# Products and running sums of the later modulation: from VectorE to ScalarE and GpSimd

## The chip, the cores and the metric

The kernel runs on one core of one Trainium2 chip. A core has five engines with a queue each: TensorE (PE, matrix products; its weight loads are shown apart as PEld), VectorE (DVE), ScalarE (ACT), GpSimd (POOL) and SyncE (SP), which here issues nearly all DMA transfers. Every engine executes its queue in order. Matrix products are written to PSUM; the other data lie in SBUF.

The metric is the time of one execution on the device, in microseconds (us); lower is better.

## What is computed

Two decoder layers over 512 tokens of width 2048, in float32. Both take shift, scale and gate from a conditioning vector `c`; the matrices for this are the *modulation* matrices. Cut to what matters:

```python
def reference(x, c, w_mod, b_mod, ...):
    c_act = jax.nn.silu(c)
    for l in range(DEPTH):                                  # 2 layers
        mod = c_act @ w_mod[l] + b_mod[l]                   # (1, 2048) @ (2048, 6144)
        shift, scale, gate = jnp.split(mod, 3, axis=-1)
        h = x * (1.0 + scale[:, None]) + shift[:, None]
        if l < N_A:                                         # layer 0
            y = diff_attention(h, a_w_in[l], a_w_out[l], ...)
        else:                                               # layer 1
            if kv is None:
                kv = shared_kv(x, c_act, kv_w_mod, kv_b_mod, kv_w, kv_b_f)
            k_sh, v_sh, F_sh = kv
            y = forgetting_attention(h, b_w_in[l - N_A], b_w_out[l - N_A], k_sh, v_sh, F_sh)
        x = layer_norm(DN_ALPHA * x + gate[:, None] * y, ln_g[l], ln_b[l])
    return x
```

`shared_kv` has a modulation of its own (`c_act @ kv_w_mod`, 2048 x 4096). A modulation is a vector times a matrix: each of the 2048 rows of the matrix is scaled by one number and the rows are added up.

## The kernel before

**Projections.** Nearly all of the time is matrix products of 512 tokens with weight matrices, done by `group`. The weights of a projection of 512 columns come in eight pairs of k-tiles (a k-tile is 128 of the 2048 rows). `WeightStream` loads a pair into `wst` (four buffers, L46, issued on SP), ScalarE rounds it to a shorter float `whi` (L93), and VectorE forms the rest `wlo = wst - whi` (L94); each of the two has three buffers. A product is then three matmuls (L173, L174, L175): upper by upper, upper by lower, lower by upper. For every pair, `group` goes over four blocks of tokens or features (`burst`: six matmuls); so a projection has 32 bursts. After a burst, `tick` takes one step of waiting work out of the list `pieces` (the attention of the head before) and, where `bg` says so, one step of `background`.

**The modulation.** The shift and scale of layer 0 are needed first and are found in the start stage (L476 and around it, up to about 165 us); that part is not edited. All later modulation goes through `mod_stream`, twice:

- the first stream, in layer 0: its gate, the shift and scale of `shared_kv` and the shift of layer 1, 16 segments of 512 columns. Tiles `ms` of two k-tiles (512 KB), two buffers, one loaded ahead;
- the second stream, during the shared values and keys (`vj[1]` to `vj[3]`, then `kj[0]` to `kj[3]`): the scale and gate of layer 1, 8 segments. Tiles `ms` of one k-tile (256 KB), three buffers, two loaded ahead.

A segment has 16 steps, one for each k-tile: VectorE multiplies a 128x512 tile with a column of silu(c) (`cact`, one number a partition) and adds it to `macc` in one instruction (L386); the first step of a segment only multiplies (L384). `macc` has two buffers. When a segment is summed, `mod_row` rounds it into `mhi` (ScalarE, L168) and `mlo` (VectorE, L169), two matmuls with ones add up its 128 partitions (L406, L407), VectorE adds the bias (L408), and the row goes to DRAM (L409).

`bg` takes a step after every second burst in the `vg` projections, after two of three in `qk`, `vj[2]`, `vj[3]` and `kj`, and after every burst in the last 17 of `vj[1]`. So the first stream has 24 - 8 = 16 segments, 256 steps, and the second 8 segments, 128 steps.

**Order.** SP takes the loads of `ms` (L369), of the weights (L46) and the stores of values (L978) in one queue. A load into a buffer that is still in use holds up those behind it. Each step of `mod_stream` first issues the load for a later step and then computes its own. The text gives priorities; the order on each engine is set when the program is compiled, by a planner that goes by estimated times and free buffers, except on VectorE in the start stage, where the order is as written.

**Work around the streams that the prediction speaks of.** In layer 0 the attention of a head runs in pieces between the bursts: scores, maximum on VectorE (L699), exponential on ScalarE (L703), transposes (L720), values, then `norm`: ScalarE copies the output (L746) and squares it (L749), VectorE takes a reciprocal root in about ten small steps (L246 to L255) and scales `og` (L753), and TensorE transposes `og` (L767). In the values' projections ScalarE copies each result into `vt` (two buffers, L977), which SP stores to DRAM (L978); there are four such copies at the end of each projection. The keys' projections copy into tiles of their own (L971) and store nothing.

Of the kernel before, what the change touches and what calls it, by code (L numbers as in the profile page):

```python
# [12 lines left out]
AF = mybir.ActivationFunctionType  # L13
ALU = mybir.AluOpType
# [4 lines left out]
T = 512  # L19
# [8 lines left out]
# Order of the start, see there: c sums of modulation, m their columns, t a k-tile of h, l its lower part,  # L28
# s a split of weights, g products of a k-tile, digits so many steps of the modulation's sums.
# [4 lines left out]
class Job:  # L34
    """A projection: runs of columns of a 2048-row weight matrix."""
# [14 lines left out]
class WeightStream:  # L50
    """Loads weights two k-tiles at a time and splits them into two float32r parts, ahead of their
    products."""
# [26 lines left out]
    def step(self, extra=None):  # L79
        """Splits the next two k-tiles; extra gives tiles for them outside the stream's own."""  # L80
        job, s = self.order[self.done]
        self.load(self.done + 1)
        st = self.stage[self.done]
        w = job.width
        if extra:
            hi, lo = ([extra() for _ in range(2)] for _ in range(2))
            for k in range(2):
                self.nc.scalar.copy(hi[k][:, :w], st[:, k, :w])
                self.nc.vector.tensor_tensor(lo[k][:, :w], st[:, k, :w], hi[k][:, :w].bitcast(F32), op=ALU.subtract)
        else:  # L90
            hi = self.pool.tile([P, 2, 512], F32R, name="whi", tag="whi", bufs=3)
            lo = self.pool.tile([P, 2, 512], F32R, name="wlo", tag="wlo", bufs=3)
            self.nc.scalar.copy(hi[:, :, :w], st[:, :, :w])  # L93
            self.nc.vector.tensor_tensor(lo[:, :, :w], st[:, :, :w], hi[:, :, :w].bitcast(F32), op=ALU.subtract)  # L94
            hi, lo = ([t[:, k, :] for k in range(2)] for t in (hi, lo))
        self.subs[(id(job), s)] = (hi, lo)
        self.done += 1
# [12 lines left out]
def tile_yoco(  # L110
# [24 lines left out]
    V, S, PE, G = nc.vector, nc.scalar, nc.tensor, nc.gpsimd  # L135
# [35 lines left out]
    def products(dst, lhs, rhs, start, stop):  # L171
        """dst += lhs^T rhs with lhs and rhs as (hi, lo) parts."""
        PE.matmul(dst, lhs[0], rhs[0], start=start, stop=False)  # L173
        PE.matmul(dst, lhs[0], rhs[1], start=False, stop=False)  # L174
        PE.matmul(dst, lhs[1], rhs[0], start=False, stop=stop)  # L175

    # ---------------------------------------------------------------- constants
# [11 lines left out]
    # rows of parameters, turned into columns by the tensor engine  # L189
# [51 lines left out]
    def rsqrt(y, v, n, pool):  # L241
        """y = v ** -0.5 by Newton steps from an estimate on the exponent."""
# [14 lines left out]
    # ---------------------------------------------------------------- weight order  # L257
# [3 lines left out]
    # the first two heads: all but the keys of the second component, which follow for both at once  # L261
    first = {h: (Job(a_w_in, [(256 * h, 256), (2048 + 256 * h, 128)]), vg[h]) for h in range(2)}
    kk = Job(a_w_in, [(2048 + 128, 128), (2048 + 384, 128)])
    # k-tiles whose modulation is found together, and the order in which the two heads take k-tiles
# [6 lines left out]
    # the last columns for half of the tokens first, whose LayerNorm is then done ahead of the end  # L271
# [34 lines left out]
    def group(job, natural, evac, banks=range(4), bg=0, before_sub=None, after_sub=None, hold=0, after_held=None):  # L306
        """One projection; natural: tokens on the partitions, else features. The last hold weights
        stay until each bank has had them, one bank after the other."""
# [41 lines left out]
    # modulation vectors as columns [feature, k-tile]  # L350
# [4 lines left out]
    def mod_stream(segs, new_stage, new_acc, nk):  # L355
        """Vector-engine products of silu(c) with columns of a modulation matrix, 512 columns a
        segment; yields after each k-tile."""
# [17 lines left out]
        for k, (i, r) in enumerate(todo):  # L375
# [4 lines left out]
            for kk in range(nk):  # L380
                kt = nk * r + kk
                w = t[:, kk, :] if nk > 1 else t
                if kt == 0:
                    V.tensor_scalar(acc, w, cact[:, 0:1], None, op0=ALU.mult)  # L384
                else:
                    V.scalar_tensor_tensor(acc, w, cact[:, kt : kt + 1], acc, op0=ALU.mult, op1=ALU.add)  # L386
                if kt == KT - 1:
                    summed.append(segs[i][2](acc))
                if kt in (1, 5) and summed:
                    if next(summed[0], None) is None:  # L390
                        summed.pop()
                yield
# [3 lines left out]
    def mod_row(pool, ones_r, dst, bias, one):  # L396
        """Sums over the partitions, as ones^T acc with acc in two parts; in two steps."""
# [14 lines left out]
    # ---------------------------------------------------------------- start: modulation and first projections  # L412
    # Shift and scale of sets of k-tiles: sums over silu(c) on the vector engine, for the first sets
    # half of them on the tensor engine. Each k-tile is multiplied for both heads; a head's partial
    # sums wait in SBUF while the other one's are in PSUM.
    part = {}
    with tc.tile_pool(name="start", bufs=2, reuse_waits="tile") as sp, tc.manual_schedule(engines={ET.DVE}):
# [12 lines left out]
        # one entry a tile: set, first k, number of k  # L430
# [53 lines left out]
        def dv(n):  # L484
            """n more products of modulation, none of them past the set after those summed."""
# [138 lines left out]
    # ---------------------------------------------------------------- layer 0: differential attention  # L624
# [182 lines left out]
    # head 1 waits until head 0 is done, and with it the values and gates of head 2  # L807
# [29 lines left out]
    # ---------------------------------------------------------------- output projections and LayerNorm  # L837
# [12 lines left out]
    def out_projection(jobs, layer, zp, opened, residual, norm, after_held=None):  # L850
        """z = residual + gate * y with the statistics of its rows; norm(b) follows a block's last
        columns. zp is filled by opened() once the pieces of the last head have been traced."""
# [43 lines left out]
    # h = x1 * scale + shift on n^T: x1 = n * g + b  # L896
# [19 lines left out]
    def build_half(s, half):  # L916
        """k-tiles 2s and 2s+1 of h for the keys and values, tokens of one half."""
# [17 lines left out]
        # the transposed tokens take the place of the others  # L935
# [3 lines left out]
    # the first values: the tokens of the second half are behind those of the first, which are ready earlier  # L939
# [25 lines left out]
    # ---------------------------------------------------------------- shared keys, values and forget gates  # L965
# [18 lines left out]
    # for each k-tile 64 columns: the two parts of the weights in columns 0-15 and 32-47. The products  # L984
    # take 128 columns, of which those 64 count.
# [26 lines left out]
    def forget_sums():  # L1012
        """-cumsum(min(z, 0) - log1p(exp(-|z|)))"""
# [6 lines left out]
        # log1p(e) = log(w) + (e - (w - 1)) / w  # L1020
# [63 lines left out]
    # ---------------------------------------------------------------- layer 1: forgetting attention  # L1084
# [4 lines left out]
    # the last block of keys is multiplied from query 256 on, so that its rows have 256 columns  # L1089
# [127 lines left out]
    # ---------------------------------------------------------------- layer 1: output projection and LayerNorm  # L1217
# [81 lines left out]
```

## Time and profile before

| | |
|---|---|
| time, median of 3 runs | 2016.39 us (2015.3 to 2018.02) |
| profiled execution, first to last instruction | 2017.1 us |
| mean granted TensorE clock | 0.994 of full speed |
| steps of `mod_stream` on VectorE | 360 of 750 ns and 24 of 485 ns |
| loads of `ms` | 128 of 512 KB (first stream), 128 of 256 KB (second) |
| first and last step, both streams | start at 176.7 and at 1320.5 us |

The page of the profile gives the busy time of each engine over the execution and, in further views, over any stretch. A row of a group reads: line, engine, operation, output<-inputs, shape, count, then busy time in all and the mean of one in ns, then how long the engine stood idle just before these instructions and what ended that. Waits are given as total us, number, longest. TensorE's busy time is modelled from its issue, so the number of matmuls in a stretch tells more than the share. The lines themselves are in the prediction.

### The profile page before, as it was taken

How to read it: one execution, taken by the hardware profiler on the slowest of the kernel's cores; microseconds unless marked ns; L12 is line 12 of the kernel's file. 1: busy time of each engine (PE TensorE's matmuls, PEld its weight loads, DVE VectorE, ACT ScalarE, POOL GpSimd, SP SyncE). 2: the span in 40 equal slices, each digit the busy share in tenths (PEclk: the TensorE clock that was granted, in tenths of full speed). 3: DMA queues.
4: the chain of work that ended last, by engine and by line, in shares of the span. 5: the costliest groups of instructions: out<-in, count | busy, mean ns of one | idle time of the engine just before them, and what ended most of it. 6: DMA issues, size and time to landing. Idle time of an engine off the chain costs nothing.

```text
span 2017.1 us, 25055 instructions
## 1 busy us (share of the span) xinstructions
PE 1967.3 (98%) x9115; PEld 1627.0 (81%) x9115; DVE 1335.3 (66%) x2435; ACT 722.2 (36%) x1230; POOL 2.2 (0%) x10
## 2 busy tenths in 40 slices
PE   5999999999999999999999999999999999999997
PEld 4888878888878888888878877888888888888885
DVE  6887878777667677853575666645455555576678
ACT  2422444423333334431263222224333333453232
POOL 0000000000000000000000000000000000000000
PEclk8999999999999999999999999999999999999999
DMA  9994755564556565452344878733233323232754
GB/s 343 343 316 143 243 172 162 163 224 156 190 167 209 166 221 184 156 165 94 115 138 141 260 255 261 261 124 127 92 102 96 103 91 103 95 118 90 259 193 175
DMA packets 263095, 353.79 MB, mean 175 GB/s; under 512 B 18022, under 2 KB 162556, under 8 KB 262204
## 3 DMA queue, kind: packets, MB, share of 16 engines
q1 hardware_dynamic: 262896, 352.18, 53.3%
q8 instruction: 71, 1.16, 0.2%
q14 instruction: 52, 0.43, 0.1%
q10 hardware_dynamic: 76, 0.02, 0.0%
HBM read 339.47 MB, written 12.66 MB: 175 GB/s over the span
## 4 chain that ended last, share of the span: by engine, by line
PE 81%; DMA 8%; DVE 8%; issue 1%; SPq 1%; ACT 1%; DVEq 0%; ACTq 0%
PE acc L173 23%; PE acc L175 23%; PE acc L174 23%; DMA ms<-in_w_mod_dram 5%; DVE macc L386 2%; DVE wlo L94 2%; PE sc L174 2%; PE sc L175 2%; PE sc L173 2%; DMA sms<-in_w_mod_dram 1%; PE o L175 1%; PE o L174 1%; PE o L173 1%; PE tr L1163 1%; DMA ms<-in_kv_w_mod_dram 1%
## 5 line engine op out<-in xcount | busy, mean ns | idle before, releaser
L93 ACT CAST whi<-wst 128x1024 fp32r<-128x1024 f32 (+2 forms) x339 | 349.6, 1032 | 685.4 <-PE acc L175 315.6
L94 DVE TENSOR_TENSOR wlo<-wst,whi 128x1024 fp32r<-128x1024 f32 (+2 forms) x339 | 404.6, 1196 | 279.9 <-ACT whi L93 265.7
L173 PE MATMUL acc<-whi,hh 128*128 128x512 f32 x1252 | 494.6, 398 | 4.4 <-ACT vt L977 2.9
L174 PE MATMUL acc<-wlo,hh 128*128 128x512 f32 x1252 | 490.6, 392 | 0.1
L175 PE MATMUL acc<-whi,hl 128*128 128x512 f32 x1252 | 489.5, 391 | 0.0
L173 PE MATMUL acc<-hh,whi 128*128 128x512 f32 x1184 | 469.0, 396 | 3.6 <-ACT vt L977 2.9
L174 PE MATMUL acc<-hl,whi 128*128 128x512 f32 x1184 | 462.3, 390 | 0.0
L175 PE MATMUL acc<-hh,wlo 128*128 128x512 f32 x1184 | 462.3, 390 | 0.0
L386 DVE SCALAR_TENSOR_TENSOR macc<-ms,cact,macc 128x512 f32<-128x512 f32 x360 | 270.0, 750 | 116.2 <-DMA ms<-in_w_mod_dram 83.7
L173 PEld LDWEIGHTS acc<-whi,hh 128*128 128x128 f32 x1252 | 236.3, 189 | 51.5 <-ACT vt L977 4.2
L175 PEld LDWEIGHTS acc<-whi,hl 128*128 128x128 f32 x1252 | 235.8, 188 | 51.1 <-DVE hl L934 0.3
L174 PEld LDWEIGHTS acc<-wlo,hh 128*128 128x128 f32 x1252 | 236.2, 189 | 44.3 <-DVE wlo L94 0.5
L173 PEld LDWEIGHTS acc<-hh,whi 128*128 128x128 f32 x1184 | 222.6, 188 | 48.4 <-ACT vt L977 4.1
L175 PEld LDWEIGHTS acc<-hh,wlo 128*128 128x128 f32 x1184 | 222.5, 188 | 48.0
L174 PEld LDWEIGHTS acc<-hl,whi 128*128 128x128 f32 x1184 | 222.8, 188 | 41.1
L476 DVE SCALAR_TENSOR_TENSOR sacc<-sms,cact,sacc 128x512 f32<-128x512 f32 (+1 forms) x127 | 89.5, 705 | 5.9 <-DMA sms<-in_w_mod_dram 2.2
L1152 ACT ACTIVATE eb<-eb,mnb 128x128 f32<-128x128 f32 (+1 forms) x64 | 36.1, 564 | 96.7 <-DVE mnb L1149 95.6
L703 ACT ACTIVATE e<-e,mn 128x128 f32<-128x128 f32 (+3 forms) x64 | 36.1, 563 | 88.7 <-DVE mn L699 88.1
L1149 DVE CUSTOM_DVE_ANT_0 eb<-sc,biasb 128x128 f32<-128x128 f32 (+1 forms) x64 | 31.4, 490 | 52.8 <-PE sc L175 52.8
L1167 DVE TENSOR_TENSOR pTl<-tr,pTh 128x128 fp32r<-128x128 f32 (+1 forms) x64 | 31.2, 487 | 26.5 <-ACT pTh L1166 26.1
L1166 ACT CAST pTh<-tr 128x128 fp32r<-128x128 f32 (+1 forms) x64 | 27.1, 424 | 43.6 <-PE tr L1163 42.9
L769 ACT ACTIVATE ogT<-tr,subg 128x128 f32<-128x128 f32 x64 | 20.0, 364 | 56.0 <-PE tr L767 56.0
(251 smaller groups left out, 1740.0 us busy)
## 6 DMA issues: line engine op xcount, KB each, us to landing
wst<-in_a_w_in_dram SPq DMA_DIRECT2D x240, 256.0 KB
ms<-in_w_mod_dram SPq DMA_DIRECT2D x64, 512.0 KB
ms<-in_kv_w_mod_dram SPq DMA_DIRECT2D x64, 512.0 KB
wst<-in_kv_w_dram SPq DMA_DIRECT2D x64, 512.0 KB
ms<-in_w_mod_dram SPq DMA_DIRECT2D x128, 256.0 KB
wst<-in_b_w_in_dram SPq DMA_DIRECT2D x128, 256.0 KB
sms<-in_w_mod_dram SPq DMA_DIRECT2D x56, 512.0 KB
wst<-in_b_w_out_dram SPq DMA_DIRECT2D x48, 512.0 KB
```

Source lines behind the costliest of these rows:

```text
L93: self.nc.scalar.copy(hi[:, :, :w], st[:, :, :w])
L94: self.nc.vector.tensor_tensor(lo[:, :, :w], st[:, :, :w], hi[:, :, :w].bitcast(F32), op=ALU.subtract)
L173: PE.matmul(dst, lhs[0], rhs[0], start=start, stop=False)
L174: PE.matmul(dst, lhs[0], rhs[1], start=False, stop=False)
L175: PE.matmul(dst, lhs[1], rhs[0], start=False, stop=stop)
L386: V.scalar_tensor_tensor(acc, w, cact[:, kt : kt + 1], acc, op0=ALU.mult, op1=ALU.add)
L476: V.scalar_tensor_tensor(acc, w, sc, acc, op0=ALU.mult, op1=ALU.add)
L703: S.activation(e[:, :w], e[:, :w], AF.Exp, bias=mn, scale=-1.0, accum_out=rs)
L1149: V.tensor_tensor_reduce(out=e[:, :w], in0=sc[:, :w], in1=bias[:, :w], scale=-1.0, scalar=3.0e38, op0=ALU.add, op1=ALU.min, accum_out=mn)
L1152: S.activation(e[:, :w], e[:, :w], AF.Exp, bias=mn, scale=-1.0, accum_out=rs)
L1166: S.copy(pTh[:, 0 : i + 1, ts], src)
L1167: V.tensor_tensor(pTl[:, 0 : i + 1, ts], src, pTh[:, 0 : i + 1, ts].bitcast(F32), op=ALU.subtract)
```

## The change

In `mod_stream`, ScalarE forms the product, in place of the loaded tile, and GpSimd adds it to `macc`. The first product of a segment is written to `macc` by ScalarE. Loads, buffers, `mod_row`, the order of the text and all else stay; the rest of the diff takes out comments.

```diff
@@ mod_stream
             for kk in range(nk):
                 kt = nk * r + kk
                 w = t[:, kk, :] if nk > 1 else t
                 if kt == 0:
-                    V.tensor_scalar(acc, w, cact[:, 0:1], None, op0=ALU.mult)
+                    S.activation(acc, w, AF.Copy, scale=cact[:, 0:1])
                 else:
-                    V.scalar_tensor_tensor(acc, w, cact[:, kt : kt + 1], acc, op0=ALU.mult, op1=ALU.add)
+                    S.activation(w, w, AF.Copy, scale=cact[:, kt : kt + 1])
+                    G.tensor_tensor(acc, acc, w, op=ALU.add)
                 if kt == KT - 1:
                     summed.append(segs[i][2](acc))
```

## The prediction

> **What bounds the kernel now.** I read the page first, then the stretches of the two streams that the change touches, then TensorE's waits in them, then who waits for the modulation's tiles, then the chain.
>
> ```profile
> span 2017.1 us, 25055 instructions
> ...
> PE 1967.3 (98%) x9115; PEld 1627.0 (81%) x9115; DVE 1335.3 (66%) x2435; ACT 722.2 (36%) x1230; POOL 2.2 (0%) x10
> ```
>
> TensorE is idle for 50 us in all, about 22 of them in the first stretch, ahead of any edited line. VectorE is off the bound on average, and so the 282 us that leave it are not a gain of that size. By stretch (span, then PE, PEld, DVE, ACT, POOL busy, clock, DMA share, GB/s):
>
> ```profile
> 0.00:50.00 50.00, 28.34 (x126) 22.91 (x127) 34.83 (x63) 11.78 (x15) 1.60 (x9) 0.90 1.02 343
> ...
> 160.00:400.00 240.00, 235.95 (x1128) 194.94 (x1127) 183.25 (x408) 100.98 (x217) 0.56 (x1) 1.00 0.56 180
> 400.00:640.00 240.00, 238.47 (x1109) 197.92 (x1109) 162.42 (x307) 82.06 (x152) 0.00 (x0) 1.00 0.59 190
> 640.00:860.00 220.00, 219.60 (x1041) 182.85 (x1040) 164.72 (x347) 88.68 (x176) 0.00 (x0) 1.00 0.56 181
> ...
> 1090.00:1180.00 90.00, 87.07 (x384) 70.94 (x383) 57.52 (x70) 21.26 (x26) 0.00 (x0) 1.00 0.75 242
> 1180.00:1250.00 70.00, 67.14 (x294) 54.55 (x293) 45.61 (x58) 16.45 (x19) 0.00 (x0) 1.00 0.80 260
> 1250.00:1330.00 80.00, 80.00 (x353) 65.94 (x352) 52.85 (x69) 21.54 (x25) 0.00 (x0) 1.00 0.72 238
> ```
>
> The first row is that start. The first stream (layer 0) runs in the next three rows, the second in the last three. TensorE's idle time is 4.05 + 1.53 + 0.40 = 6.0 us in the first and 2.93 + 2.86 + 0 = 5.8 us in the second. These 11.8 us are the most that the change can win. Three views of TensorE's waits (165 to 400, 540 to 600, 1085 to 1250 us) name them:
>
> ```profile
> PE tr L767 <- DVE og L753: 3.1, 3, 1.3
> ...
> PE tr L767 <- DVE og L753: 1.0, 1, 1.0
> ...
> PE acc L173 <- ACT vt L977: 5.8, 5, 2.7
> ```
>
> In layer 0 it is VectorE, late with the gated head `og`: 4.1 us. In the second stream it is ScalarE, late with `vt`; the views of all waits, and the same for 1060 to 1330 us, say why:
>
> ```profile
> ACT vt L977 <- DMA v_dram<-vt: 16.2, 4, 7.4
> DVE macc L386 <- DMA ms<-in_w_mod_dram: 83.7, 69, 3.4
> DVE macc L386 <- DMA ms<-in_kv_w_mod_dram: 26.3, 28, 3.2
> ...
> DVE macc L386 <- DMA ms<-in_w_mod_dram: 61.0, 45, 3.4
> ...
> SPq L369 <- DVE macc L386: 166.2, 189, 4.6
> ```
>
> `vt` has two buffers; the third copy waits for the store of the first, and that store stands on SP's queue behind loads of `ms` (L369) that wait for VectorE to free a buffer. So the second stream's TensorE time is already lost to the ring of `ms` buffers: load, use, free, load. VectorE itself stood 110.0 us waiting for `ms`, 61.0 of them in the second stream. In layer 0 the chain shows what that does (start, us, what):
>
> ```profile
> 261.29 1.22 DVE wlo L94
> ...
> 263.79 4.64 DMA ms<-in_w_mod_dram
> 268.45 0.75 DVE macc L386
> ...
> 273.41 0.50 DVE og L753
> ...
> 274.05 0.41 PE tr L767 x2
> ```
>
> The sum stands 4.64 us for its tile at VectorE's head, the small steps of `og` stand behind it, and TensorE behind them.
>
> **The change, part by part.** It removes 360 fused steps and 24 first products from VectorE:
>
> ```profile
> L386 DVE SCALAR_TENSOR_TENSOR macc<-ms,cact,macc 128x512 f32<-128x512 f32 x360 | 270.0, 750 | 116.2 <-DMA ms<-in_w_mod_dram 83.7 <-DMA ms<-in_kv_w_mod_dram 26.3 <-DVE mn L699 0.3
> L384 DVE TENSOR_SCALAR macc<-ms,cact 128x512 f32<-128x512 f32 x24 | 11.6, 485 | 6.0 <-DMA ms<-in_w_mod_dram 5.5
> L94 DVE TENSOR_TENSOR wlo<-wst,whi 128x1024 fp32r<-128x1024 f32 (+2 forms) x339 | 404.6, 1196 | 279.9 <-ACT whi L93 265.7 <-DMA vld<-v_dram 8.4 <-DMA wst<-in_kv_w_dram 2.5
> ```
>
> That is 281.6 us. It adds 384 products on ScalarE and 360 sums on GpSimd. No row has either; the nearest are these:
>
> ```profile
> L168 ACT CAST mhi<-macc 128x512 fp32r<-128x512 f32 x24 | 14.9, 620 | 40.4 <-PE tr L406 23.3 <-DVE macc L386 17.1
> L769 ACT ACTIVATE ogT<-tr,subg 128x128 f32<-128x128 f32 x64 | 20.0, 364 | 56.0 <-PE tr L767 56.0
> L1166 ACT CAST pTh<-tr 128x128 fp32r<-128x128 f32 x16 | 4.2, 264 | 7.1 <-PE tr L1163 6.9
> L522 ACT ACTIVATE htmp<-tr,mcol 128x512 f32<-128x512 f32 x16 | 12.3, 770 | 0.0
> ...
> L646 POOL IOTA dist<- 128x512 f32 x1 | 0.6, 560 | 158.7 <-DVE sacc L476 158.7
> ```
>
> *A product.* The copy of such a tile takes 620 ns; a scale taken from a column costs 364 - 264 = 100 ns more. I take 0.72 us, between 0.62 and the 0.77 of an instruction with two such columns. In all 276 us. In layer 0 ScalarE goes from 101 + 82 + 89 = 272 us of 700 to 272 + 256 x 0.72 = 456 (65%), VectorE from 510 to 510 - 256 x 0.75 = 318; in the second stream ScalarE goes from 59 of 240 to 151. Neither is full, so as sheer work the products are hidden behind TensorE; uncovered, they would cost their 276 us.
>
> *A sum.* GpSimd's only row of the size is the IOTA, one pass of writing: 0.56 us. An add reads two operands and writes one. Below I put one pass (0.56, all overlapped), above three (1.68), and take two, 1.12: two operands as two passes, the write beside them. 360 x 1.12 = 403 us on an engine with 2.2 us of work. [...]
>
> *What moves.* The product overwrites its tile, so a buffer is free after product and sum, not after one fused step. On ScalarE the wait for a tile now stands ahead of the splits `whi` (L93), the exponentials (L703), `og`'s evacuation (L746, L749) and `vt`; VectorE waits for `whi`, TensorE for both. On SP the loads L369 wait for GpSimd; behind them stand the weights' loads (L46) and the stores of `vt` (L978). `mhi` waits for GpSimd's last sum.
>
> *The ring.* The chain in the second stream, and the tile's first and last steps there:
>
> ```profile
> 1127.95 5.36 DMA ms<-in_w_mod_dram
> 1133.41 0.76 DVE macc L386
> 1134.19 4.55 DMA ms<-in_w_mod_dram
> 1138.83 0.76 DVE macc L386
> 1139.61 3.59 DMA ms<-in_w_mod_dram
> ...
> 1145.87 4.60 DMA ms<-in_w_mod_dram
> ...
> L386 DVE SCALAR_TENSOR_TENSOR macc<-ms,cact,macc x120: 732/752/755, 1102.7 to 1320.5; 128x512 f32<-128x512 f32 x120
> L384 DVE TENSOR_SCALAR macc<-ms,cact x8: 468/481/489, 1098.0 to 1294.6; 128x512 f32<-128x512 f32 x8
> ```
>
> A load lands (5.36 + 4.55 + 3.59 + 4.60) / 4 = 4.53 us after its buffer is free; with the step 5.29 us for three buffers, 1.76 us a step. The whole stream bears it out: 128 steps from 1098.0 to 1320.5 us, 1.74 each. Afterwards: 4.53 + 0.72 + 1.12 + 0.1 for one more handover (in these rows landing to step is 0.1) = 6.47, or 2.16 us a step; with the bounds 5.81 (0.62 and 0.56) to 7.08 (0.77 and 1.68), 1.94 to 2.36. What TensorE's program asks: a matmul starts every 80 / 353 = 0.227 us, a group has 32 x 6 of them (43.5 us) and 21 steps, so 2.07 us a step, and 1.36 in the 17 steps of `vj[1]`. The ring, now quicker than the program, becomes slightly slower.
>
> In layer 0 two buffers hold two steps each: 4.64 (the row above) + 0.72 + 2 x 1.12 + 0.2 = 7.8 us for four steps, 1.95 each, where 256 steps in 700 us have 2.7. That ring stays in front.
>
> *The sum.* Layer 0: the 4.1 us of waits for `og` go, but 110.0 - 61.0 = 49 us of waits for tiles now stand ahead of the evacuation that feeds `og`; I let a third come back: -2.7 (between -6.0 and, with ScalarE's delays as long as VectorE's were and as much again, +6). Second stream: each of the five waits for `vt` grows with the ring by 6.47 - 5.29 = 1.18 us: +5.9. In the `kj` groups 69 steps lose 0.09 each, 6.2, of which 5.4 are covered by one pair of k-tiles split ahead (24 matmuls): +0.8. So 2017.1 - 2.7 + 6.7 = 2021.1. The profiled execution is 0.7 above the median 2016.39, inside the runs' 2015.3 to 2018.0; I say 2021.
>
> **The rivals.**
>
> *Relief wins.* The sums may run ahead of or behind the program by two segments (`macc` has two buffers), nothing needs the last rows (layer 1's gate) before the last projection, and the 2.16 can fall to 1.94, under 2.07. Then the ring is hidden and TensorE regains 4.1 us and some 2 of the `vt` waits: 2010. For it: no wait of TensorE for `mhi` or `mlo` in its three views. Against: the 5.8 us come through SP's queue, which the change makes wait longer.
>
> *VectorE and GpSimd hold each other up.* Place: the second stream. If a sum that meets a split `wlo` (1196 ns) stands for half of it, the ring is 6.47 + 0.6 = 7.07, 2.36 us a step, and 111 steps lose (2.36 - 2.07) x 111 = 32 us, less 5.4 covered, plus 5 x 1.78 at `vt`, less 2.7: +33, so 2050. It decides once the ring passes 6.2 us, what the program has for three steps; each 0.3 beyond costs some 11 us. For it: three sums and a split fall in each 5.4 us. Against: no row shows two engines sharing a port, and VectorE has 36% free there (57.52 of 90 busy). [...]
>
> *Nothing moves.* TensorE is 98% busy and no stretch loses over 4 us; gain and loss cancel: 2016.
>
> **How the numbers follow.** The forecast has 0.45, relief 0.30, the hold-up 0.17, nothing 0.08. A measurement here can tell 0.2%, 4 us, from no change. Faster: most of relief and a little of nothing, 0.29. Same (2012.4 to 2020.4): 0.09 of the forecast, 0.03 of relief, 0.06 of nothing, 0.18. Slower: 0.36 of the forecast and the hold-up, 0.53. The forecast's own range is 2015 to 2031. The range reaches down to 2008, below which is a third of relief, and up to 2044, above which is most of the hold-up.
>
> **What would show it.** Right: no L386 on VectorE; a product near 0.72 us; sums spaced 1.1 us or more; TensorE's waits for `og` under 2 us; waits for `vt` near 12 us; the second stream ending near 1375, not 1320. Wrong: the time of free to landing shrinks once loads are issued singly; `wlo` well above 1.2 us (the hold-up); ScalarE's waits for `ms` over 110 us with TensorE waiting at `whi` in layer 0, which no case prices above +6; the stream ending by 1330.

## The result, and the profile after

The changed kernel takes 2140.4 us (median of 4 runs, 2139.01 to 2141.7), and the kernel before took 2017.2 us in runs on the same chip (2015.3 to 2019.65): a ratio of 1.060, 95% interval 1.059 to 1.0615. The change makes the kernel 6% slower. The prediction had the sign right (slower) and the size wrong: 2021 us, with a range up to 2044.

First the page of the changed kernel: span, busy time by engine, the chain that ended last, and the groups that answer to those of before.

```profile
span 2137.8 us, 25842 instructions
...
PE 2004.7 (94%) x9115; PEld 1642.9 (77%) x9115; DVE 1175.9 (55%) x2051; ACT 961.7 (45%) x1614; POOL 493.3 (23%) x370
...
PE 52%; DMA 16%; issue 12%; POOL 10%; DVE 5%; ACT 4%; SPq 1%; POOLq 0%; ACTq 0%; DVEq 0%
PE acc L173 15%; PE acc L175 14%; PE acc L174 14%; POOL macc L387 10%; DMA ms<-in_w_mod_dram 10%; DMA ms<-in_kv_w_mod_dram 5%; ACT ms L386 3%; PE sc L173 1%; PE sc L174 1%; PE sc L175 1%; DVE wlo L94 1%; PE tr L1164 1%; PE o L175 1%; PE o L
...
L94 DVE TENSOR_TENSOR wlo<-wst,whi 128x1024 fp32r<-128x1024 f32 (+2 forms) x339 | 451.0, 1333 | 553.1 <-ACT whi L93 512.2
L387 POOL TENSOR_TENSOR macc<-macc,ms 128x512 f32<-128x512 f32 x360 | 491.1, 1364 | 792.4 <-ACT ms L386 495.6
...
L386 ACT ACTIVATE ms<-ms,cact 128x512 f32<-128x512 f32 x360 | 249.7, 719 | 295.2 <-DMA ms<-in_w_mod_dram 185.4
```

The chain that ended last, before:

```profile
PE 81%; DMA 8%; DVE 8%; issue 1%; SPq 1%; ACT 1%; DVEq 0%; ACTq 0%
PE acc L173 23%; PE acc L175 23%; PE acc L174 23%; DMA ms<-in_w_mod_dram 5%; DVE macc L386 2%; DVE wlo L94 2%; PE sc L174 2%; PE sc L175 2%; PE sc L173 2%; DMA sms<-in_w_mod_dram 1%; PE o L175 1%; PE o L174 1%; PE o L173 1%; PE tr L1163 1%;
```

TensorE's share of the chain fell from 81% to 52%, and GpSimd, idle before, has 10%. By line, the ring of `ms` (load, product, sum) now has 10 + 10 + 5 + 3 = 28% of the chain; before, its loads and the fused step had 5 + 2 = 7% in the rows shown. Three more things stand out. The product on ScalarE costs what was forecast (719 ns). The sum on GpSimd costs 1364 ns and not 1120. And VectorE, which gave up 281.6 us of work, is busy only 1335.3 - 1175.9 = 159.4 us less: other instructions of it have become 122.2 us longer in all, though nothing in them was edited. `wlo` alone accounts for 451.0 - 404.6 = 46.4 us of that.

Which others, the view of VectorE's groups by line says, before and after (the line numbers move by one: L711 is L712, L753 is L754, L708 is L709). The kernel before:

```profile
L711 DVE SCALAR_TENSOR_TENSOR e<-e,rsum 128x128 f32<-128x128 f32 (+3 forms) x32 | 17.6, 549 | 0.6
...
L753 DVE SCALAR_TENSOR_TENSOR og<-og,rstd,sg 128x256 f32<-128x256 f32 x32 | 14.1, 480 | 0.6
...
L254 DVE TENSOR_TENSOR rs_a<-rs_a,rs_h 128x2 f32<-128x2 f32 x48 | 7.6, 158 | 0.9
...
L708 DVE TENSOR_TENSOR rsum<-rsum,neglam 128x1 f32<-128x1 f32 x32 | 5.0, 156 | 0.5
```

The changed kernel:

```profile
L712 DVE SCALAR_TENSOR_TENSOR e<-e,rsum 128x128 f32<-128x128 f32 (+3 forms) x32 | 27.6, 861 | 1.0
...
L754 DVE SCALAR_TENSOR_TENSOR og<-og,rstd,sg 128x256 f32<-128x256 f32 x32 | 20.5, 681 | 0.8
...
L709 DVE TENSOR_TENSOR rsum<-rsum,neglam 128x1 f32<-128x1 f32 x32 | 15.1, 470 | 0.9
...
L254 DVE TENSOR_TENSOR rs_a<-rs_a,rs_h 128x2 f32<-128x2 f32 x48 | 11.8, 247 | 1.3
```

These are steps of the attention in layer 0, most of them small. L709 handles one number in each partition and takes three times as long on average. A mean hides how that comes about; the durations of single instructions (min/median/max in ns) show it, first in the view of the tile `rsum`:

```profile
L708 DVE RECIPROCAL rsum<-rsum x32: 146/166/168, 249.0 to 947.5; 128x2 f32<-128x2 f32 x32
L709 DVE TENSOR_TENSOR rsum<-rsum,neglam x32: 151/184/1250, 249.2 to 947.7; 128x1 f32<-128x1 f32 x32
```

then of `rs_a`, a step of the root (its longest was 163 before):

```profile
L254 DVE TENSOR_TENSOR rs_a<-rs_a,rs_h x48: 148/161/1284, 270.5 to 960.5; 128x2 f32<-128x2 f32 x48
```

and of `macc`, with GpSimd's sums:

```profile
L387 POOL TENSOR_TENSOR macc<-macc,ms x360: 1261/1294/2263, 180.1 to 1444.5; 128x512 f32<-128x512 f32 x180
```

Most of these steps take their usual 0.16 to 0.18 us, and a few take up to 1.28 us: as long as one sum of GpSimd (median 1.294). The reciprocal L708, with one operand and as small, never does. And one stretch of the timeline (start, us, engine, line) has the two side by side:

```profile
263.93 5.72 POOL L387 TENSOR_TENSOR macc<-macc,ms 128x512 f32<-128x512 f32 x4 [2.48 <-ACT ms L386]
...
264.63 0.61 DVE L709 TENSOR_TENSOR rsum<-rsum,neglam 128x1 f32<-128x1 f32 x1
...
265.60 1.51 DVE L712 SCALAR_TENSOR_TENSOR e<-e,rsum 128x384 f32<-128x384 f32 x1
...
267.25 0.52 PE L721 MATMUL tr<-ident,e 128*128 128x128 f32 x3 [1.47 <-DVE e L712]
...
268.39 1.28 DVE L248 TENSOR_SCALAR rs_h<-ss 128x2 f32<-128x2 f32 x1
...
271.35 1.30 POOL L387 TENSOR_TENSOR macc<-macc,ms 128x512 f32<-128x512 f32 x1 [1.71 <-ACT ms L386]
271.39 1.28 DVE L254 TENSOR_TENSOR rs_a<-rs_a,rs_h 128x2 f32<-128x2 f32 x1
```

The last two rows are the cleanest: a sum runs from 271.35 to 272.65; a VectorE step on two numbers a partition starts 0.04 us behind it and ends at 272.67, 0.02 us after it. In the rows above them L712 takes 1.51 us (0.615 on average for this shape before), and TensorE waits 1.47 us for it. It goes the other way as well: the longest sum, 2263 ns where the median is 1294, runs from 1368.66 to 1370.92 us; it starts 0.08 us behind a `wlo` of 1.23 us and ends 1.11 us after it.

Where TensorE lost its time, the windows tell (span, then PE, PEld, DVE, ACT, POOL busy, clock, DMA share, GB/s):

```profile
160.00:400.00 240.00, 217.48 (x1001) 176.08 (x1000) 147.07 (x287) 137.40 (x269) 103.31 (x76) 0.98 0.55 168
400.00:640.00 240.00, 219.00 (x1008) 176.90 (x1007) 121.22 (x229) 127.37 (x238) 102.05 (x75) 0.99 0.52 163
640.00:860.00 220.00, 201.71 (x905) 164.80 (x904) 101.06 (x196) 108.98 (x199) 85.14 (x62) 0.96 0.50 155
...
1240.00:1360.00 120.00, 108.39 (x455) 88.27 (x454) 34.62 (x26) 64.43 (x89) 69.88 (x54) 0.93 0.71 224
1360.00:1480.00 120.00, 108.46 (x455) 87.92 (x454) 37.64 (x34) 59.25 (x81) 57.33 (x43) 0.94 0.58 181
```

In the 700 us of layer 0 from 160 us on TensorE stands still for 22.5 + 21.0 + 18.3 = 61.8 us, where it was 6.0 before. Two markers divide the whole difference: the start of the last copy of `n` (L912, now L913), at the end of layer 0, and of the last copy of `kT` (L971, now L972), at the end of the keys.

| start of the last | before | after | later by |
|---|---|---|---|
| copy of `n` | 1024.8 us | 1114.7 us | 89.9 us |
| copy of `kT` | 1395.4 us | 1516.6 us | 121.2 us |

Layer 0 lost 89.9 us, the stretch of the second stream 121.2 - 89.9 = 31.3 us; together 121.2, to half a microsecond the difference of the spans (120.7).

Finally the waits (total us, number, longest) over the whole span:

```profile
ACT ms L386 <- DMA ms<-in_w_mod_dram: 185.4, 129, 5.1
...
ACT ms L386 <- DMA ms<-in_kv_w_mod_dram: 100.4, 56, 4.1
...
PE tr L721 <- DVE e L712: 17.2, 11, 4.0
...
PE acc L173 <- DVE q0l L658: 13.8, 5, 5.0
...
PE tr L768 <- DVE og L754: 6.9, 2, 5.3
```

of SP's queue:

```profile
SPq L369 <- POOL macc L387: 429.1, 234, 4.4
```

and TensorE's alone in the stretch from 1240 to 1480 us, in the second stream, where these two rows are all there is:

```profile
PE acc L173 <- ACT vt L978: 11.6, 3, 6.8
PE acc L173 <- ACT kT L972: 11.5, 3, 5.9
```

All of TensorE's waits in the first of these views, smaller rows included, add up to 118.9 us, where they were 35.7 before: 83.2 more, all of the 83.3 us by which its idle time grew (2137.8 - 2004.7 against 2017.1 - 1967.3). Those ended by VectorE grew from 22.5 to 80.4 us, those ended by ScalarE from 10.7 to 35.9. The three rows of VectorE shown (`e`, `q0l`, `og`) are steps of layer 0: VectorE, which was relieved, is what TensorE waits for there. In the second stream it is ScalarE: 11.6 + 11.5 = 23.1 us for `vt` and `kT`, the whole of TensorE's idle time in the last two windows above (11.6 + 11.5). ScalarE's own timeline says why, here just before TensorE starts again at 1371.7 us after a wait of 5.3:

```profile
1370.46 0.72 ACT L386 ACTIVATE ms<-ms,cact 128x512 f32<-128x512 f32 x1 [1.92 <-DMA ms<-in_w_mod_dram]
1371.09 0.57 ACT L972 COPY kT<-acc 128x512 f32<-128x512 f32 x1
```

The copy that TensorE waits for stands in ScalarE's queue behind a product that waits for its tile. It is the same at the three other long waits of the stretch: they end at 1265.7, 1318.8 and 1424.2 us, after 4.5, 6.8 and 5.9 us, and a product just ahead of the copy in the queue had stood 1.70, 2.12 and 3.18 us for its load. SP's loads of `ms` now stand 429 us for GpSimd, where they stood 166 us for VectorE. The other 37.4 of the 120.7 us are TensorE being busy longer, at a mean granted clock of 0.978 instead of 0.994.

### The profile page after: what moved, and what is told of

Its sections match the earlier page's. It is cut to its first block, busy times and chain, and to the rows that moved or that the text cites. A ratio compares the mean times of both kernels' runs of the same rounds, so it can differ in the third digit from the quotient of the medians.

```text
span 2137.8 us, 25842 instructions
## 1 busy us (share of the span) xinstructions
PE 2004.7 (94%) x9115; PEld 1642.9 (77%) x9115; DVE 1175.9 (55%) x2051; ACT 961.7 (45%) x1614; POOL 493.3 (23%) x370
## 4 chain that ended last, share of the span: by engine, by line
PE 52%; DMA 16%; issue 12%; POOL 10%; DVE 5%; ACT 4%; SPq 1%; POOLq 0%; ACTq 0%; DVEq 0%
PE acc L173 15%; PE acc L175 14%; PE acc L174 14%; POOL macc L387 10%; DMA ms<-in_w_mod_dram 10%; DMA ms<-in_kv_w_mod_dram 5%; ACT ms L386 3%; PE sc L173 1%; PE sc L174 1%; PE sc L175 1%; DVE wlo L94 1%; PE tr L1164 1%; PE o L175 1%; PE o L173 1%; PE o L174 1%
## 5 line engine op out<-in xcount | busy, mean ns | idle before, releaser
L94 DVE TENSOR_TENSOR wlo<-wst,whi 128x1024 fp32r<-128x1024 f32 (+2 forms) x339 | 451.0, 1333 | 553.1 <-ACT whi L93 512.2
L387 POOL TENSOR_TENSOR macc<-macc,ms 128x512 f32<-128x512 f32 x360 | 491.1, 1364 | 792.4 <-ACT ms L386 495.6
L173 PE MATMUL acc<-whi,hh 128*128 128x512 f32 x1252 | 502.6, 404 | 29.0 <-DVE q0l L658 13.8
L173 PE MATMUL acc<-hh,whi 128*128 128x512 f32 x1184 | 473.8, 400 | 27.4 <-ACT kT L972 11.5
L386 ACT ACTIVATE ms<-ms,cact 128x512 f32<-128x512 f32 x360 | 249.7, 719 | 295.2 <-DMA ms<-in_w_mod_dram 185.4
```

The source lines that it names most:

```text
L386: S.activation(w, w, AF.Copy, scale=cact[:, kt : kt + 1])
L387: G.tensor_tensor(acc, acc, w, op=ALU.add)
```

## The experiments

Three theories stood at the start. **T1**: the product itself, on ScalarE: it stands for its tile at the head of ScalarE's queue, ahead of `whi` and the attention. **T2**: the ring of `ms` buffers: a buffer is free only after product and sum, the loads come late. **T3**: GpSimd and VectorE hold each other up. All times below have their ratio to the kernel before, run on the same chip.

**Which half of the change costs?** First the product on ScalarE with the sum back on VectorE:

```diff
-                    G.tensor_tensor(acc, acc, w, op=ALU.add)
+                    V.tensor_tensor(acc, acc, w, op=ALU.add)
```

> Product on ScalarE as in the change, sum on VectorE instead of GpSimd. Three theories. (T1) ScalarE now stands at the head of its queue until a tile of ms has landed, with whi, the exponentials and the evacuations behind it: then most of the loss stays, 2085 us or more, and ScalarE's waits for ms stay over 200 us. (T2) The ring of ms buffers has become too long, whoever waits: it is 4.5 + 0.72 + 0.69 = 5.9 us for three steps of the second stream, about half way between before (5.3) and the change (6.6): 2060 to 2080. (T3) GpSimd and VectorE hold each other up: GpSimd has no work here, so 2015 to 2030.

2033.07 us, 1.0076 (1.0061 to 1.0091): 3 us above T3's range and far below the others. Its groups and waits:

```profile
L387 DVE TENSOR_TENSOR macc<-macc,ms 128x512 f32<-128x512 f32 x360 | 248.5, 690 | 152.1 <-ACT ms L386 132.5 <-ACT macc L384 4.7 <-DVE macc L387 1.4
L386 ACT ACTIVATE ms<-ms,cact 128x512 f32<-128x512 f32 x360 | 248.0, 720 | 202.8 <-DMA ms<-in_w_mod_dram 124.6 <-DMA ms<-in_kv_w_mod_dram 70.2 <-DVE macc L387 3.6
```

ScalarE stands 124.6 + 70.2 = 195 us for its tiles here, `wlo` has its old 1196 ns, and the kernel loses 15 us. The product on ScalarE, its waits, and a buffer held some 0.7 us longer are all in this run: T1 by itself is not what costs 123 us. Then the other half, the product on VectorE and the sum on GpSimd:

```diff
-                    S.activation(acc, w, AF.Copy, scale=cact[:, 0:1])
+                    V.tensor_scalar(acc, w, cact[:, 0:1], None, op0=ALU.mult)
...
-                    S.activation(w, w, AF.Copy, scale=cact[:, kt : kt + 1])
+                    V.tensor_scalar(w, w, cact[:, kt : kt + 1], None, op0=ALU.mult)
```

> Product on VectorE (in place, a single operand and a column), sum on GpSimd as in the change. The ring is as long as in the change to 0.25 us, but VectorE waits for the tiles, as before, and ScalarE has no work of the modulation. T1: 2060 us or less. T2: 2120 to 2145. T3: 2110 or more, since the sums on GpSimd are all there, and wlo stays over 1.3 us.

2181.79 us, 1.0808 (1.079 to 1.0826). ScalarE is as before, and the time is worse than the change's: T1's 2060 or less is missed, T2's 2120 to 2145 is passed, and T3's 2110 or more holds. GpSimd's sum is what both slow kernels have in common.

**Where?** The change in the first stream alone, the second as before (the first product of a segment is divided in the same way):

```diff
...
-                else:
+                elif nk > 1:
                     S.activation(w, w, AF.Copy, scale=cact[:, kt : kt + 1])
                     G.tensor_tensor(acc, acc, w, op=ALU.add)
+                else:
+                    V.scalar_tensor_tensor(acc, w, cact[:, kt : kt + 1], acc, op0=ALU.mult, op1=ALU.add)
```

> The change in the first stream alone (layer 0); the second stream as before. By the times at which the same instructions run in the two traces, layer 0 ends 90 us later and the second stream adds 31. If the two losses stand for themselves: 2107 us (2100 to 2115). If the second stream's loss hangs on the first (it starts late, or with its queues behind): under 2030 is not possible, but 2125 or more is, or 2080 if part of the first is made good where slack is left. No theory is told apart; it says how much each stream has to explain.

2108.96 us, 1.0451 (1.0432 to 1.0469): 2140.4 - 2109.0 = 31 us fall to the second stream and the rest to the first, just as the two markers divide it and within the 2100 to 2115 expected if the two losses stand for themselves.

**Is it the ring?** The change with tiles `ms` of one k-tile in the first stream, four buffers and three loads ahead (as many bytes as before):

```diff
...
-        lambda: ap.tile([P, 2, 512], F32, name="ms", tag="ms", bufs=2),
+        lambda: ap.tile([P, 512], F32, name="ms", tag="ms", bufs=4),
...
-        2,
+        1,
+        3,
```

> The change, with the first stream's ring in the same space: four buffers of one k-tile, three loaded ahead, instead of two buffers of two k-tiles. A buffer is free after one product and one sum; the ring gives a step every (4.5 + 0.72 + 1.3) / 4 = 1.6 us instead of (4.6 + 0.72 + 2.7) / 4 = 2.0. T2: most of layer 0's 90 us come back: 2060 or less. T1: ScalarE's waits for ms fall with the ring and so does the loss, but only as far as those waits do: 2070 to 2110. T3: the sums are as many and as long: 2130 or more.

2102.16 us, 1.042 (1.0403 to 1.0437): 38 us are won back, and most of the loss stays. Both T2 (2060 or less) and T3 (2130 or more) missed; the time lies in the range of T1, and ScalarE's waits for `ms` fell with it, from 286 to 226 us. So the ring has a share in the change's loss. The same in both streams (the second with four buffers instead of three):

> The change with four buffers of one k-tile in the first stream (2102 us) and also four, three ahead, in the second. Its ring then gives a step every (4.5 + 0.72 + 1.3) / 4 = 1.6 us, under the program's 2.07. T2: the second stream's 34 us come back, 2065 to 2075. T3: 2095 or more.

2098.3 us, 1.0394 (1.0378 to 1.0409). Under T2 the second stream should have regained much of its 31 us, and it regained 4: a miss for T2, while T3's 2095 or more holds. These shorter rings with the sum on VectorE, and the unchanged kernel with these rings:

> Product on ScalarE, sum on VectorE, with both rings of four single k-tiles: the same as the change with these rings (2098 us) but for the engine of the sum. If what those 2098 us have over the 2017 of before is GpSimd and VectorE holding each other up: 2015 to 2028. If ScalarE standing for tiles has a share that short rings don't take away: 2035 or more.

> The kernel before, both steps in one on VectorE, with both rings of four single k-tiles, three ahead. If the ring costs TensorE some of its 11.8 us of idle time in the streams already before: 2007 to 2014. If the ring of before is just long enough: 2015 to 2020. If twice as many loads in layer 0 crowd SP's queue: over 2022.

2019.15 us, 1.0018 (1.0008 to 1.0027), and 2018.02 us, 1.001 (1.000 to 1.002). With equal buffers the sum on GpSimd costs 79.2 - 2.9 = 76 us more than on VectorE, each loss taken against the kernel before on its own chip (2019.07 and 2016.27 us). In the kernel before, the second stream's waits for `vt`, which the prediction put down as "already lost to the ring", were still 5.1 us with the shorter ring (5.8 before): a shorter ring gives nothing back there.

**The ring alone, longer.** A small store of each tile on GpSimd's queue holds the buffer after its last use; first in the kernel before, then in the kernel of the first experiment:

```diff
+    hold_dram = dram.tile([1, 16], F32, name="hold_dram")
...
+                if kk == nk - 1:
+                    G.dma_start(hold_dram[:, :], w[0:1, 0:16])
```

> The kernel before, with its fused step on VectorE; each tile of ms is also read by a small store of 64 bytes to DRAM, issued on GpSimd's queue after the tile's last step, so that its buffer comes free some 2 us later, as it does in the change (a product of 0.72 and sums of 1.3 in place of a step of 0.75: 1.3 us a step in the second stream, 1.9 a tile in the first). No GpSimd arithmetic, ScalarE as before. T2 (ring): 2090 or more, VectorE's waits for ms at 230 us or more. T3: 2015 to 2035.

> Product on ScalarE, sum on VectorE (2033 us), with the same small store holding each tile some 2 us longer. ScalarE stands for the tiles, the ring is as long as in the change or longer, GpSimd computes nothing. T2 with ScalarE at the head (ring and T1 together): 2120 or more. T3: 2030 to 2060.

2250.27 us, 1.1153 (1.1129 to 1.1176), and 2302.49 us, 1.1405 (1.1386 to 1.1423). The hold came out longer than the change's: the stores waited for each other, 806 us on GpSimd's queue in the first of the two, and VectorE stood 396 us for `ms` (ScalarE 543 in the second), against 286 in the change. Both times are on T2's side of the expectations. They show that a ring can cost this much when it is long enough, with `wlo` at 1195 ns and no hold-up at all; they don't say what the change's own ring costs.

**The hold-up alone.** The kernel before, fused step and all, with 360 more sums of the change's size on GpSimd, one behind each fused step. They touch no buffer of `ms`, and what they write is read in the two streams by eight `bias` steps of VectorE alone, which waited 1.2 us for it in all:

```diff
-                    V.scalar_tensor_tensor(acc, w, cact[:, kt : kt + 1], acc, op0=ALU.mult, op1=ALU.add)
+                    done = V.scalar_tensor_tensor(acc, w, cact[:, kt : kt + 1], acc, op0=ALU.mult, op1=ALU.add)
+                    m4 = mask.rearrange("p (a n) -> p a n", a=4)
+                    one4 = ones.rearrange("p (a n) -> p a n", a=1).broadcast_to([P, 4, P])
+                    extra = G.tensor_tensor(m4, m4, one4, op=ALU.mult)
...
+                    tc.add_manual_dep(extra.ins, done.ins.name, info, reason="pace")
```

> The kernel before, with its fused step on VectorE, and beside each of the 360 steps a sum of the same shape on GpSimd that nothing waits for (the mask times one, in place; it starts when the step on VectorE is done and holds no ms buffer). So GpSimd is as busy as in the change, the ring and ScalarE are as before. T3 (GpSimd and VectorE hold each other up): wlo at 1.3 us or more instead of 1.2, L711 and the small steps of the root longer, and a good part of the loss, 2050 us or more. T2 (ring) and T1: 2015 to 2030. The product over all 360 has no other reader than the bias steps, once for each head.

2182.81 us, 1.0813 (1.0795 to 1.0831). Its groups:

```profile
L389 POOL TENSOR_TENSOR mask<-mask,ones 128x512 f32<-128x512 f32 x360 | 617.6, 1716 | 716.9 <-DVE macc L386 553.1 <-DVE bias L691 54.6 <-DVE rs_a L254 53.1
...
L94 DVE TENSOR_TENSOR wlo<-wst,whi 128x1024 fp32r<-128x1024 f32 (+2 forms) x339 | 478.8, 1416 | 242.7 <-ACT whi L93 237.6 <-DMA vld<-v_dram 2.8 <-DMA ms<-in_w_mod_dram 0.8
...
L386 DVE SCALAR_TENSOR_TENSOR macc<-ms,cact,macc 128x512 f32<-128x512 f32 x360 | 423.0, 1175 | 39.3 <-DMA ms<-in_w_mod_dram 33.3
```

164 us are lost, although VectorE stands only 39 us ahead of the fused step (116 before), ScalarE's work is untouched and, those 1.2 us aside, nothing waits for a sum. TensorE, VectorE and ScalarE execute their 9115, 2435 and 1230 instructions in exactly the order of the kernel before, so the planner's order has no share in it either. The fused step of 750 ns takes 1175 here, `wlo` 1416 instead of 1196, the sum 1716. The hold-up alone is enough for a loss larger than the change's, as T3 had it (2050 or more). It isn't the change's own amount: of VectorE's 1625.3 - 1335.3 = 290 us of standing, 423.0 - 270.0 = 153 are those of the fused step, which the change doesn't have.

**Shorter sums.** If a VectorE step stands until the running sum ends, halving the sums halves the longest wait:

```diff
-                    G.tensor_tensor(acc, acc, w, op=ALU.add)
+                    for hs in (slice(0, 256), slice(256, 512)):
+                        G.tensor_tensor(acc[:, hs], acc[:, hs], w[:, hs], op=ALU.add)
```

> The change, with each sum on GpSimd cut into two of 256 columns. If an instruction of VectorE stands until the running sum of GpSimd is done, it now stands for half of one: L254 (two columns) has its longest at 0.9 us or less instead of 1.28, and the time falls: 2085 to 2125. If the length of GpSimd's work or of the ring decides, which grows by one more start (some 0.1 us a step): 2140 to 2165.

2170.8 us, 1.0761 (1.0744 to 1.0779). The durations of the small step:

```profile
L254 DVE TENSOR_TENSOR rs_a<-rs_a,rs_h x48: 152/161/668, 269.0 to 983.1; 128x2 f32<-128x2 f32 x48
```

and of the halves:

```profile
L388 POOL TENSOR_TENSOR macc<-macc,ms x720: 716/738/1787, 176.7 to 1474.9; 128x256 f32<-128x256 f32 x180
```

The longest wait of the small step fell from 1284 to 668 ns, as T3 has it. The time rose nevertheless, above both expectations (2085 to 2125 for T3, 2140 to 2165 if the length of GpSimd's work or of the ring decides): two halves take 2 x 0.827 (their mean) = 1.65 us a step instead of 1.364, ScalarE's waits for tiles grew from 286 to 306 us, and VectorE's busy time fell by only 20 us. The mechanism showed, and halving is no remedy; the run doesn't separate T2 from T3.

**The sum out of the ring.** ScalarE writes the product to a tile of its own, so that a buffer of `ms` is free after the product, and the sum holds no load. There is one such tile (with tiles `ms` of one k-tile, three buffers, in both streams):

```diff
...
-                    S.activation(w, w, AF.Copy, scale=cact[:, kt : kt + 1])
-                    G.tensor_tensor(acc, acc, w, op=ALU.add)
+                    pr = new_prod()
+                    S.activation(pr, w, AF.Copy, scale=cact[:, kt : kt + 1])
+                    G.tensor_tensor(acc, acc, pr, op=ALU.add)
```

> The change, but ScalarE writes the product to a tile of its own (one buffer) and no longer over the loaded tile, and the tiles ms are of one k-tile with three buffers in both streams. So a buffer of ms is free after the product, as it was after VectorE's fused step before, and GpSimd's sum is out of the ring of loads; it stays on the chip at the same time as VectorE. The same two streams with the sum on VectorE and four buffers took 2019 us, with the sum on GpSimd 2098. If what GpSimd costs beyond that 2019 is the longer hold of the buffers (T2), this kernel comes to 2015 to 2035 us. If it is the two engines holding each other up (T3), the loss stays: 2080 to 2125 us, wlo above 1.28 us on average, a root step of two columns still up to 1.1 us or more, while the loads on SP wait for ScalarE and hardly for GpSimd. With one product tile ScalarE can wait for GpSimd's sum; up to 30 us of such waits on ScalarE are expected, and more than 80 us would blur the reading.

2196.7 us, 1.0886 (1.0867 to 1.0904): outside both expectations. ScalarE stood 342 us for the one product tile, so a third wait had come in, and the run decides nothing. With two product tiles (`mhi` takes turns with them in the same two), the sum on GpSimd and, as a control, on VectorE:

```diff
...
-            hi = pool.tile([P, 512], F32R, name="mhi", tag="mhi", bufs=1)
+            hi = pool.tile([P, 512], F32R, name="mhi", tag="pr", bufs=2)
```

> As the run before (product in a tile of its own, tiles ms of one k-tile with three buffers), with two product tiles, one of them shared with mhi, which rounds a finished segment. ScalarE should then stand for GpSimd under 80 us, not 342. If what GpSimd costs is mostly the hold of the loaded tiles (T2), the sum on GpSimd is now within 25 us of the sum on VectorE (the next kernel). If it is the two engines holding each other up (T3), it is 55 to 110 us above it, with wlo at 1.28 us or more against 1.20.

> The control: the same buffers and products, the sum on VectorE. Both theories: 2015 to 2040 us, wlo 1.20, no root step of two columns over 0.17 us. Above 2060 the product tiles themselves cost time and only the difference to the kernel before in this call counts.

2163.54 us, 1.0725 (1.0704 to 1.0745), and 2012.69 us, 0.9974 (0.9965 to 0.9983). The product's waits with the sum on GpSimd:

```profile
ACT pr L387 <- POOL macc L388: 306.4, 266, 3.6
...
ACT pr L387 <- DMA ms<-in_w_mod_dram: 30.5, 22, 3.5
```

With the sum on VectorE these waits are 118.5 and 43.4 us.

The loads are now never late for long (30 us of waits for this matrix instead of 185), and the sum on GpSimd costs more than ever, 151 us against the control: over T2's 25 us, and over the 55 to 110 of T3 as well. So the hold of the loaded tiles is not a condition of the loss, which speaks against T2. ScalarE, though, still stood 306 us, far over the 80 that the expectation allowed, so this run doesn't give the hold-up's amount either; what a slow sum keeps waiting is now ScalarE itself. `wlo` takes 1265 ns on average here, less than the 1333 in the change, although the loss is larger. The control is the one version faster than the kernel before, by 5 us (0.26%), and it keeps one half of the change: the product on ScalarE. Part of the gain is that of the short tiles: with the sum on VectorE they alone brought the loss from 15 to 3 us.

| what holds the loaded tile, buffers | sum on VectorE | sum on GpSimd | difference of the losses, each against the kernel before on its chip |
|---|---|---|---|
| product and sum, as in the change | 2033.07 us | 2140.4 us | 108 us |
| product and sum, four short buffers | 2019.15 us | 2098.3 us | 76 us |
| product only, two product tiles | 2012.69 us | 2163.54 us | 151 us |

**What is settled, and what isn't.** In three arrangements of the buffers the product on ScalarE costs between -5 and +15 us, and the sum on GpSimd 76 to 151 us on top. That VectorE's steps stand until a running sum ends is shown by single rows, and that this alone can cost as much, by the kernel whose extra sums hardly anything waits for. How the change's 108 us divide between that and the slow sum's being waited for (through the ring, by ScalarE) stays open: each run that took one away brought another wait in. In the change's own trace 58 of the 83 us that TensorE lost to waiting were ended by VectorE, nearly all in layer 0, and 25 by ScalarE, in the second stream above all. In the second stream the way is clear from the rows: the copies of `vt` and `kT` stand behind products that wait for their tiles, and no VectorE step is waited for. In layer 0 it is not: a VectorE step can also be late because its input was. One more thing is untested. The planner put some instructions in another order when the sum changed its engine (54 of the 2051 VectorE steps common to the change and the first experiment stand elsewhere), and no run moves the sum and keeps the order.

## Why the prediction was wrong, step by step

- **The price of a product** (0.72 us): right, 0.719. That it is hidden as work: right; with the sum on VectorE it costs 15 us or less.
- **The price of a sum** (1.12 us, between 0.56 and 1.68): inside the bounds, too low: at least 1.261, median 1.294, mean 1.364.
- **Layer 0, "-2.7", and "That ring stays in front"**: the step that failed most, by 93 us. The ring's length was about right: 7.8 us for four steps were forecast, and the chain of waits around 230 to 247 us, below, has cycles of 9.4 and 7.8 (from one load's start to the next's). But it was set against the mean of 2.7 us a step, and the upper end (+6) let ScalarE's delays grow to no more than twice VectorE's 49 us. In the stretch below, sixteen products start between 225.8 and 257.9 us, one every 2.0 us: there the ring sets the pace. ScalarE waited 189 us for tiles in layer 0 (286 in all), and TensorE's waits for `og` went up to 6.9 us instead of away.

```profile
229.70 5.05 DMA ms<-in_w_mod_dram
...
234.84 0.73 ACT ms L386
...
235.69 2.00 POOL macc L387
...
237.76 1.29 POOL macc L387
...
239.06 4.14 DMA ms<-in_w_mod_dram
...
246.84 3.73 DMA ms<-in_w_mod_dram
```

- **The hold-up as a rival with 0.17**: a mechanism that is there, put in the wrong place and priced at +33 us where the whole loss was 123. It was put into the second stream, with half a `wlo` on the ring; TensorE waits for no VectorE step there. Where TensorE does wait for VectorE is layer 0, and the steps held there were not counted at all because they are small: a step of 0.16 us that stands 1.28 us, one of about ten in a row ahead of `og`. The argument against it, that VectorE has 36% free, weighs nothing there: a held step lies on a chain whatever the engine's share is.
- **Second stream, +6.7**: measured +31.3. The ring came out no slower than forecast: 128 steps from 1186.3 to 1443.7 us are one every 2.01 us, and not 2.16. Its sums were longer (1.364 and not 1.12), its loads shorter: in the chain that ended last, 33 of them took 3.70 us on average, where 18 took 4.15 before and the prediction took 4.53 from four. What failed is the path. The waits for `vt` were to grow through the stores, but ScalarE's waits for the stores fell from 16.2 to 4.9 us; the waits for `vt` came to 15.5 us, where some 12 were forecast, and the two longest of them (4.5 and 6.8 us) ended with a copy that stood behind products that waited for their tiles. The 11.5 us for `kT`, which come the same way, were put at nothing, since the keys store nothing. And TensorE ran at a granted clock of 0.93 in this stretch where it had 1.00, which no term held.
- **Of the signs named beforehand**, three that were to show the forecast wrong did: `wlo` well above 1.2 us (1.33), ScalarE's waits for `ms` over 110 us (286) with TensorE standing in layer 0, and, by less, a shorter time of a load (3.70 against 4.15 us in the second stream, as above, and 4.00 for 46 loads of the chain in layer 0 against 4.72 for 9 before). The second stream's products ended at 1443.7 us and not near 1375, because layer 0 came late: the stream itself took 257 us, where 277 (1375 - 1098) were forecast.
- **The chances**: 0.53 for slower was the right side; the range ended at 2044 because no case priced layer 0 above +6 us.

## What to carry to other kernels

Work moved from VectorE to GpSimd was not off VectorE here: of 281.6 us moved, 122.2 came back as longer steps. While adds of GpSimd ran (median 1.29 us), steps of VectorE with two operands in SBUF stood, in the rows above one of 0.16 us for 1.28 us, to the end of the add, and one with a single operand stood as long (L248); so count those steps on the chains that feed TensorE, the smallest first, and price each at up to one whole GpSimd instruction. Look at the longest duration of such a step, not at its mean or at an engine's free share. Ask as well what else stands in the queue that gets the wait for a load: here it was the copies of TensorE's results into `vt` and `kT`, for which TensorE waited 23.1 us. If a fused step has to be split over two engines, short tiles and a tile of its own for the first result let the load's buffer come free sooner (with the sum on VectorE, ScalarE waited 43.4 us for the tiles of `w_mod` and not 124.6); with the sum there, single k-tiles in four buffers brought a loss of 15 us to 3, and single k-tiles with two product tiles made it a gain of 5.

## What the runs showed of the hardware that was not expected

- **An add of 128x512 float32 on GpSimd** takes 1294 ns (median), one of 128x256 738 ns: (1294 - 738) / 256 = 2.17 ns a column and about 0.18 us beside. VectorE's add of the same tile took 690 ns in the first experiment.
- **Which steps are held**: L709, L254 and L712, with two tensors in SBUF, are (the longest 1.25, 1.28 and 1.65 us, where before they were 0.16, 0.16 and 0.75); a reciprocal of two columns (L708) never was, in 32 instances (the longest 0.17 us); but L248, with one tensor, stood 1.28 us at 268.39 us, to the end of a run of four sums.
- **The granted clock was lower where TensorE stood more**: its mean is 0.995 in the fastest kernel here, 0.978 in the change, 0.966 with one product tile and 0.948 in the slowest. In the first three TensorE is idle for 44.6, 133.1 and 169.2 us and busy for 1965.7, 2004.7 and 2025.4 us, with the same 9115 matmuls. So the waits of the change cost more than their length: 37 of its 121 us are TensorE's longer busy time. One wait shows it in the trace, that of 6.8 us for `vt`, which ends at 1318.8 us: in the rows of the stretch around its end and of the one behind it (columns as in the windows above) the clock is 0.50 and then 1.00.

```profile
1315.00:1324.00 9.00, 5.21 (x12) 4.13 (x13) 2.37 (x3) 6.72 (x10) 4.10 (x4) 0.50 0.81 266
1325.00:1345.00 20.00, 19.66 (x87) 15.94 (x86) 4.16 (x3) 10.17 (x14) 12.51 (x9) 1.00 0.75 231
```
